# A two-layer RWKV-7 / RG-LRU trunk: the triangular solves on two engines, and their loads and merges as steps of their own

## The chip, the cores and the metric

The kernel runs on one core of a Trainium2 chip. The metric is the device time of one execution, in microseconds (us); the figure compared is the median of several executions. The engines are named as in the profile: PE (TensorE), PEld (its weight loads), DVE (VectorE), ACT (ScalarE), POOL (GpSimd) and SP (SyncE, which issues nearly all DMAs here).

## The reference

A decoder trunk of two layers on 1024 positions of width 1024, in float32. Each layer adds a token mixer, a cross attention into 256 memory rows and a squared-ReLU MLP, each between two RMS norms. Layer 0's mixer is an RG-LRU block, layer 1's is RWKV-7 time mixing, and the change lies in that one:

```python
r = (x + xx * mu[0]) @ w_rkv[0]
k = (x + xx * mu[2]) @ w_rkv[1]
v = (x + xx * mu[3]) @ w_rkv[2]
...
a = jax.nn.sigmoid(a0 + (xa @ a1) @ a2)
kk = (k * k_k).reshape(B, S, H, N).astype(jnp.float32)
kk = kk / jnp.maximum(jnp.linalg.norm(kk, axis=-1, keepdims=True), 1e-12)
k = k * (1.0 + (a - 1.0) * k_a)
...
def step(state, inp):
    r_t, w_t, k_t, v_t, a_t, b_t = inp          # a_t = -kk, b_t = kk * a
    sa = jnp.einsum('bhij,bhj->bhi', state, a_t)
    state = (state * w_t[:, :, None, :] + sa[..., None] * b_t[:, :, None, :]
             + v_t[..., None] * k_t[:, :, None, :])
    y_t = jnp.einsum('bhij,bhj->bhi', state, r_t)
    return state, y_t
```

The kernel computes this recurrence in 16 chunks of 64 positions. Within a chunk the part of `sa` that depends on earlier positions of the same chunk is a triangular system; its inverse `X` (64x64 for each of 16 heads and each chunk) is computed ahead of the scan over the chunks.

## The kernel before

Every big product is made three times with parts of the float32 operands (`split`, L193 on ACT and L194 on DVE, makes the high and low part; `mm3`, L294 to L296, the three matmuls). A scheduler orders the instructions of each engine by its own model of their times, within the dependencies of data and buffers, so an engine's order is not that of the code. Each engine and each DMA queue then works strictly in its order. All DMAs named here are issued by SP, in one queue.

The RWKV layer, around 1280 to 2000 us in the profiled execution, goes like this.

- **k, eight feature blocks** `f` = 0 to 7. `decay(f)` makes the decays (L1143 to L1152: among them the scan L1147 on DVE, the store L1151 of the running product `P`, and the copy L1152 of its last column of each chunk on POOL). `fphase` makes the 48 matmuls of 512 columns of block `f` and hands PSUM to `prep` (L1160 to L1175), which evacuates it: L1160 on ACT and L1163 on DVE read PSUM, L1166, L1171 and L1172 are three products of 128x1024 on DVE, L1168 and L1169 make `at`, L1174 and L1175 store two tensors. `sums(f-1)` (L1182 to L1193) adds squares with 16 small matmuls and sends the norms through DRAM into `db` (L1193). `gram(f-1)` (L1204 to L1212) makes 64 products of 64x64, scales them from PSUM by `db` on DVE (L1205) and stores them: `Ld` holds the diagonal 32x32 blocks, `Mod` the others. With 12 more matmuls for the decay that is 60 of 512 columns for a block.
- **r, eight blocks** in seven turns ([0] to [5], then [6, 7]). `early` loads `P` of the block (L1299), `evac_r` multiplies it by PSUM (L1303, DVE) and stores it (L1304). The mixes of `x` (`rwkv_make_mix`, L1041 on ACT, L1042 and L1044 on DVE, and a split of each of four tiles) are made in two halves, one under the last of k and one behind it; the mix of v likewise around the last turn of r.
- **v, eight blocks**, whose evacuation on DVE is L1334, and then the scan over the 16 chunks.

**The triangular part** works on pairs of blocks, `q` = 0 to 3. `solve(q)` loads 128 blocks of 32x32, one on each partition (L1217), sets `xt_` to the identity (L1219, L1220) and makes 31 steps of two operations, L1225 (a product of two broadcast views, 31 to 256 elements) and L1227 (an addition), each of which needs the one before; L1228 turns the result. `solve_store` writes it to DRAM (L1233, L1234). `merge_load` clears a tile `XT` (L1240) and reads the blocks back in another layout (L1246 to L1248, 8 DMAs a block, 16 a pair), `merge` makes the off-diagonal 32x32 blocks (matmuls L1261 and L1268, ACT copies L1263 and L1271) and stores `XT` (L1272).

`aside(step)` decides where these stand in the code: steps 0 to 7 come at the end of the turns of k, 8 to 14 of r, 15 and later of v. The tuples give for each `q` the step of a function: solves at (2, 5, 7, 10), their stores at (6, 7, 8, 11), the merge's loads at (10, 9, 11, 14) and the merges at (12, 10, 13, 16).

## Time and profile before

| what | value |
|---|---|
| median of 3 executions | 3063.79 us (3063.06 to 3066.52) |
| profiled execution | 3055.81 us, its span 3054.0 us |
| mean granted clock of TensorE | 0.97 |
| busy share of the span | PE 95%, PEld 79%, DVE 59%, ACT 44%, POOL 39% |
| instructions | 42,879 |

The span is the profiled part of one execution, from its first instruction to its last. A busy share is the time in which the engine had an instruction in work; weight loads overlap matmuls. The granted clock is 1 at 2.4 GHz and 0.5 at 1.2 GHz, so a mean between them over a stretch is a mixture of spells at either. In rows of a timeline the number behind the start is the duration, "x4" says that four like instructions stand in one row, and the bracket gives the idle time of the engine ahead of it and what ended it. "SPq" rows are the issue of DMAs by SP's queue.

### The profile page before, as it was taken

The page shows a single profiled execution, that of the slowest core. Times are in us where ns is not written, and L with a number is a line of the kernel's source. Part 1 is how long each engine was busy: PE and PEld are TensorE (multiplying, and loading weights), DVE is VectorE, ACT ScalarE, POOL GpSimd, SP SyncE. Part 2 cuts the span into 40 slices and gives each one's busy share as a digit, 9 for nine tenths or more (in the row PEclk, how much of TensorE's full clock was granted, in tenths as well). Part 3 has the DMA queues.
Part 4 walks back from the last instruction along what each step waited for, and adds up shares of the span by engine and source line. Part 5 has one row for each costly group of instructions (what it writes and reads, how often), then busy time and mean ns, then how long its engine had stood idle before and what let it go on. Part 6 is the DMA issues. An engine that isn't in the chain of part 4 may idle for free.

```text
span 3054.0 us, 42879 instructions
## 1 busy us (share of the span) xinstructions
PE 2890.0 (95%) x16987; PEld 2399.1 (79%) x16987; DVE 1788.2 (59%) x1967; ACT 1341.6 (44%) x1907; POOL 1186.4 (39%) x1096
## 2 busy tenths in 40 slices
PE   7999999898999999989977898989999899999998
PEld 6887898786888878877766777878778778887886
DVE  5576542637454787767662535884345644568776
ACT  5464342635454543346331434442334544454332
POOL 2000100015766754440677504662001466667442
PEclk9999999998999999999978999999999999999999
DMA  8213270122545554342537779862312244455443
GB/s 259 71 42 103 83 225 35 56 83 76 169 152 191 211 185 155 104 138 74 134 104 200 208 219 250 176 159 87 107 34 84 83 151 151 153 204 200 158 137 117
DMA packets 394921, 421.93 MB, mean 138 GB/s; under 512 B 103536, under 2 KB 305504, under 8 KB 394720
## 3 DMA queue, kind: packets, MB, share of 16 engines
q1 hardware_dynamic: 384720, 384.96, 42.2%
q0 software_dynamic: 9536, 33.64, 2.8%
q8 instruction: 134, 2.20, 0.3%
q14 instruction: 67, 0.55, 0.1%
q10 hardware_dynamic: 464, 0.59, 0.1%
HBM read 284.31 MB, written 134.74 MB: 137 GB/s over the span
## 4 chain that ended last, share of the span: by engine, by line
PE 49%; POOL 10%; DVE 5%; issue 5%; DMA 2%; ACT 2%; SPq 1%; POOLq 0%; DVEq 0%; ACTq 0%
PE q L294 12%; PE q L295 12%; PE q L296 12%; PE p L295 4%; PE p L296 4%; PE p L294 4%; POOL u L1227 3%; POOL u L1225 2%; DVE u L194 2%; DMA u<-d 1%; POOL u L1542 1%; ACT u L193 1%; PE q L1444 1%; DMA u<-in_b_w_rkv 1%; DVE u L1555 1%
## 5 line engine op out<-in xcount | busy, mean ns | idle before, releaser
L194 DVE TENSOR_TENSOR u<-u,u 128x1024 fp32r<-128x1024 f32 (+1 forms) x518 | 808.3, 1588 | 383.0 <-ACT u L193 358.0
L193 ACT CAST u<-u 128x1024 fp32r<-128x1024 f32 (+1 forms) x550 | 542.7, 1024 | 475.7 <-PE q L295 159.1
L294 PE MATMUL p<-u,u 128*128 128x512 f32 (+1 forms) x1920 | 720.1, 378 | 25.6 <-ACT u L193 12.2
L295 PE MATMUL p<-u,u 128*128 128x512 f32 (+1 forms) x1920 | 722.5, 376 | 9.2 <-DVE u L194 9.2
L296 PE MATMUL p<-u,u 128*128 128x512 f32 (+1 forms) x1920 | 719.8, 375 | 3.7 <-DVE u L194 3.7
L294 PE MATMUL q<-u,u 128*128 128x512 f32 (+1 forms) x1632 | 643.6, 395 | 39.1 <-DVE u L1205 16.7
L295 PE MATMUL q<-u,u 128*128 128x512 f32 (+1 forms) x1632 | 640.1, 393 | 6.2 <-DVE u L194 6.2
L296 PE MATMUL q<-u,u 128*128 128x512 f32 (+1 forms) x1632 | 634.9, 392 | 0.0
L294 PEld LDWEIGHTS p<-u,u 128*128 128x128 f32 x1920 | 369.4, 193 | 95.2 <-ACT u L193 17.0
L295 PEld LDWEIGHTS p<-u,u 128*128 128x128 f32 x1920 | 370.3, 193 | 77.1 <-DVE u L194 13.7
L296 PEld LDWEIGHTS p<-u,u 128*128 128x128 f32 x1920 | 370.0, 193 | 68.9 <-DVE u L194 5.8
L305 POOL TENSOR_SCALAR s<-s 128x1 f32<-128x1 f32 x98 | 34.4, 351 | 994.6 <-ACT u L303 993.6
L294 PEld LDWEIGHTS q<-u,u 128*128 128x128 f32 (+1 forms) x1632 | 308.9, 190 | 111.7 <-DVE u L1205 17.1
L295 PEld LDWEIGHTS q<-u,u 128*128 128x128 f32 (+1 forms) x1632 | 309.5, 190 | 71.8 <-DVE u L194 8.1
L296 PEld LDWEIGHTS q<-u,u 128*128 128x128 f32 (+1 forms) x1632 | 309.2, 189 | 65.3 <-issue 0.4
L421 POOL TENSOR_TENSOR u<-u,u 128x1024 f32<-128x1024 f32 x64 | 179.1, 2820 | 86.5 <-DVE u L194 80.4
L965 DVE TENSOR_TENSOR z<-z,q 128x512 f32<-128x512 f32 x192 | 128.7, 679 | 93.4 <-PE q L296 93.1
L194 POOL TENSOR_TENSOR u<-u,u 128x1024 fp32r<-128x1024 f32 x32 | 95.0, 2967 | 165.0 <-ACT u L193 104.0
L401 POOL TENSOR_TENSOR u<-u,u 128x512 f32<-128x512 f32 x96 | 148.2, 1553 | 2.9
L294 PE MATMUL q<-z,u 128*128 128x512 f32 x256 | 102.1, 399 | 7.0 <-DVE u L600 7.0
L916 POOL TENSOR_TENSOR u<-u,u 128x512 f32<-128x512 f32 x32 | 46.1, 1440 | 158.5 <-ACT u L905 152.4
L1225 POOL TENSOR_TENSOR u<-u,u 128x31 f32<-128x31 f32 (+15 forms) x124 | 84.9, 685 | 53.0 <-DMA u<-d 32.4
(251 smaller groups left out, 3500.0 us busy)
## 6 DMA issues: line engine op xcount, KB each, us to landing
u<-d SPq DMA_DIRECT2D x201, 512.0 KB, 4.4
d<-u SPq DMA_DIRECT2D x113, 512.0 KB, 3.5
d<-u SPq DMA_DIRECT2D x132, 256.0 KB, 3.5
u<-in_m_w_up SPq DMA_DIRECT2D x64, 512.0 KB, 5.8
d<-u POOLq DMA_DIRECT2D x64, 512.0 KB, 4.1
u<-in_m_w_down SPq DMA_DIRECT2D x64, 512.0 KB, 6.4
u<-in_c_w_kv SPq DMA_DIRECT2D x32, 512.0 KB, 6.5
u<-d SPq DMA_DIRECT2D x56, 256.0 KB, 6.1
```

What stands on the lines that cost most here:

```text
L193: self.nc.scalar.copy(hv, src)
L194: (eng or self.nc.vector).tensor_tensor(lv, src, hv, ALU.subtract)
L294: mm(o, ah, bh, start=first, stop=False, **kw)
L295: mm(o, ah, bl, start=False, stop=False, **kw)
L296: mm(o, al, bh, start=False, stop=last, **kw)
L305: nc.gpsimd.tensor_scalar(v, ss, 1.0 / n, eps, ALU.mult, ALU.add)
L401: sub = lambda o, x, y: nc.gpsimd.tensor_tensor(o, x, y, ALU.subtract)
L421: self.nc.gpsimd.tensor_tensor(f[o][i], f[x][i], f[y][i], ALU.subtract)
L916: tt(s1, r21, r22, ALU.add)
L965: nc.vector.tensor_add(to_, to_, o)
L1225: nc.gpsimd.tensor_tensor(tv, xv_[:, 0:n, s:s + 1].broadcast_to([128, n, m]), Lv[:, s:s + 1, s + 1:].broadcast_to([128, n, m]), ALU.mult)
L1227: nc.gpsimd.tensor_tensor(xv_[:, 0:n, s + 1:], xv_[:, 0:n, s + 1:], tv, ALU.add)
```

## The change

Three of the four solves, `q` = 1 to 3, go from POOL to DVE with all their operations; `q` = 0 stays on POOL (`SE`). `solve` is cut in two: `solve_load` (the load and the two memsets) and `solve`. The store of `XT` leaves `merge` and becomes `merge_store`. Each call in `aside` stands under `behind()`, which takes the last instruction in the code so far on each engine and lets the scheduler issue the call's instructions only after it. The steps are new numbers, and later ones for the stores of the solves of `q` = 0 to 3: (12, 10, 12, 14). Besides, the three products of `prep` (L1166, L1171, L1172) go from DVE to POOL, the copy L1152 from POOL to ACT, and the memset of `XT` (L1240) from POOL to DVE.

```diff
--- before.py
+++ after.py
...
+    @contextmanager
+    def behind(self):
+
+        with ExitStack() as stack:
+            if not self.rec:
+                last = {i.engine: i for i in self.nc.cur_bb.bb.instructions}
+                for i in last.values():
+                    stack.enter_context(self.tc.issue_after(i))
+            yield
 
 
     def nm(self, s):
@@ -980,7 +990,10 @@
                     rest()
 
 
-SO, ST, ML, ME = (2, 5, 7, 10), (6, 7, 8, 11), (10, 9, 11, 14), (12, 10, 13, 16)
+
+SL, SO, ST = (6, 7, 9, 11), (7, 8, 10, 12), (12, 10, 12, 14)
+ML, ME, MS = (13, 11, 13, 15), (14, 12, 14, 16), (15, 13, 15, 17)
+SE = [lambda nc: nc.gpsimd] + [lambda nc: nc.vector] * 3
 DA = (2, 1)
 LD = 6
 POST = lambda nc: nc.vector
@@ -1129,7 +1142,7 @@
     nc.gpsimd.memset(d01[:, ::64], 0.0)
     ch = lambda t: t.rearrange("p (c t) -> p c t", t=64)
     hr = [slice(0, 64), slice(64, 128)]
-    dk, st_k, mg, sol, ld, sm = {}, {}, {}, {}, {}, {}
+    dk, st_k, mg, sol, ld, sm, xts = {}, {}, {}, {}, {}, {}, {}
 
     def decay(f):
         cs = slice(f * 128, f * 128 + 128)
@@ -1149,7 +1162,7 @@
         nc.scalar.activation(P, IP, AF.Exp)
         nc.scalar.activation(IP, IP, AF.Exp, scale=-1.0)
         nc.sync.dma_start(Pd[cs, :], P)
-        nc.gpsimd.tensor_copy(self.pc.rearrange("p (c q) -> p c q", q=8)[:, :, f], P[:, 63::64])
+        nc.scalar.copy(self.pc.rearrange("p (c q) -> p c q", q=8)[:, :, f], P[:, 63::64])
         dk[f] = a, P, IP
 
     def prep(f, pk):
@@ -1163,13 +1176,13 @@
         nc.vector.tensor_mul(kp, kp, pk)
         sq = self.unit()
         nc.scalar.activation(sq, kk, AF.Square)
-        nc.vector.tensor_mul(a, a, kk)
+        nc.gpsimd.tensor_tensor(a, a, kk, ALU.mult)
         at = kk
         nc.vector.scalar_tensor_tensor(ch(at)[:, :, 1:], ch(kk)[:, :, 1:], -1.0, ch(P)[:, :, :63], ALU.mult, ALU.mult)
         nc.vector.tensor_scalar(at[:, ::64], kk[:, ::64], -1.0, None, ALU.mult)
         nc.sync.dma_start(MVd[:, f, 0, :], at)
-        nc.vector.tensor_mul(a, a, IP)
-        nc.vector.tensor_mul(kp, kp, IP)
+        nc.gpsimd.tensor_tensor(a, a, IP, ALU.mult)
+        nc.gpsimd.tensor_tensor(kp, kp, IP, ALU.mult)
         for h in range(2):
             nc.sync.dma_start(STd[hr[h], f, h, :], a[hr[h], :])
             nc.sync.dma_start(STd[hr[h], f, 1 - h, :], kp[hr[h], :])
@@ -1211,33 +1224,36 @@
                 nc.sync.dma_start(Ld[f // 2, b, f % 2, h].rearrange("c s t -> s c t"), ch(mt)[rs, :, b * 32:b * 32 + 32])
             nc.sync.dma_start(Mod[f, h], ch(mt)[h * 64:h * 64 + 32, :, 32:64])
 
+    def solve_load(q):
+        sol[q] = [self.unit() for _ in range(3)]
+        L, xt_, tmp = sol[q]
+        nc.sync.dma_start(L, Ld[q].rearrange("b q h c s t -> (b q h c) (s t)"))
+        SE[q](nc).memset(xt_, 0.0)
+        SE[q](nc).memset(xt_[:, ::33], 1.0)
+
     def solve(q):
 
-        L, xt_, tmp = (self.unit() for _ in range(3))
-        nc.sync.dma_start(L, Ld[q].rearrange("b q h c s t -> (b q h c) (s t)"))
+        L, xt_, tmp = sol[q]
+        eng = SE[q](nc)
         Lv = L.rearrange("p (s t) -> p s t", t=32)
-        nc.gpsimd.memset(xt_, 0.0)
-        nc.gpsimd.memset(xt_[:, ::33], 1.0)
         xv_ = xt_.rearrange("p (j t) -> p j t", t=32)
         for s in range(31):
             n, m = s + 1, 31 - s
             tv = tmp[:, :n * m].rearrange("p (j t) -> p j t", t=m)
-            nc.gpsimd.tensor_tensor(tv, xv_[:, 0:n, s:s + 1].broadcast_to([128, n, m]),
-                                    Lv[:, s:s + 1, s + 1:].broadcast_to([128, n, m]), ALU.mult)
-            nc.gpsimd.tensor_tensor(xv_[:, 0:n, s + 1:], xv_[:, 0:n, s + 1:], tv, ALU.add)
-        nc.gpsimd.tensor_copy(tmp[0:64].rearrange("p (s j) -> p s j", j=32), xt_[0:64].rearrange("p (j s) -> p s j", s=32))
-        sol[q] = xt_, tmp
+            eng.tensor_tensor(tv, xv_[:, 0:n, s:s + 1].broadcast_to([128, n, m]),
+                              Lv[:, s:s + 1, s + 1:].broadcast_to([128, n, m]), ALU.mult)
+            eng.tensor_tensor(xv_[:, 0:n, s + 1:], xv_[:, 0:n, s + 1:], tv, ALU.add)
+        eng.tensor_copy(tmp[0:64].rearrange("p (s j) -> p s j", j=32), xt_[0:64].rearrange("p (j s) -> p s j", s=32))
 
     def solve_store(q):
-        xt_, tmp = sol.pop(q)
+        L, xt_, tmp = sol.pop(q)
         nc.sync.dma_start(Xd[q].rearrange("b q h c s t -> (b q h c) (s t)"), xt_)
         nc.sync.dma_start(Xnd[2 * q:2 * q + 2].rearrange("q h c s t -> (q h c) (s t)"), tmp[0:64])
-
 
     def merge_load(q):
         for f in (2 * q, 2 * q + 1):
             XT = self.unit()
-            nc.gpsimd.memset(XT, 0.0)
+            nc.vector.memset(XT, 0.0)
             XN = self.unit()
             xc = ch(XT)
             for h in range(2):
@@ -1269,13 +1285,19 @@
                        start=True, stop=True, tile_position=(h * 64 + 32, h * 64))
             for h in range(2):
                 nc.scalar.copy(xc[r0[h], :, 32:64], ps[r0[h], :].rearrange("p (c t) -> p c t", t=32))
-            nc.sync.dma_start(XTd[:, f, :], XT)
+            xts[f] = XT
+
+    def merge_store(q):
+        for f in (2 * q, 2 * q + 1):
+            nc.sync.dma_start(XTd[:, f, :], xts.pop(f))
 
     def aside(step):
 
-        for fn, steps in ((solve_store, ST), (merge, ME), (merge_load, ML), (solve, SO)):
-            if step in steps:
-                fn(steps.index(step))
+        for fn, steps in ((merge_store, MS), (merge, ME), (merge_load, ML), (solve_store, ST), (solve, SO), (solve_load, SL)):
+            for q in range(4):
+                if steps[q] == step:
+                    with self.behind():
+                        fn(q)
 
     self.depth, self.ahead = DA
     xr, xv = [], []
```

The lines of the changed kernel have other numbers: L1225 and L1227 (solve) become L1243 and L1245, L1219 and L1220 (its memsets) L1231 and L1232, L1217 (its load) L1230, L1233 and L1234 (its store) L1250 and L1251, L1240 (memset of `XT`) L1256, L1246 to L1248 (loads of the merge) L1262 to L1264, L1193 (`db`) L1206, L1205 (`gram`) L1218, L1299 (load of `P`) L1321, L1303 (evacuation of r) L1325, L1304 L1326, L194 L204, L225 (weights) L235.

First place: SP's queue in the last turns of k. In the kernel before, the store of solve 0 (L1233, L1234) stands there ahead of loads of `db` (L1193):

```order
L1233 DMA d_10006<-u_10824 128x1024
L1151 DMA d_10001<-u_11214 128x1024
L1234 DMA d_10007<-u_10825 64x1024
L1193 DMA db<-d_11325 64x8 x2
L1175 DMA d_10003<-u_11310 64x1024 x2
L1170 DMA d_10002<-u_11308 128x1024
L1193 DMA db<-d_11325 64x8
```

In the changed kernel the queue of the same turns reads as follows (`d_11417` is the DRAM copy of the norms, `d_10005` is `Ld`, `d_10004` is `Mod`):

```order
L1164 DMA d_10001<-u_11306 128x1024
L1206 DMA db<-d_11417 64x8 x4
L1183 DMA d_10002<-u_11400 128x1024
L1188 DMA d_10003<-u_11402 64x1024 x2
L1224 DMA d_10005<-u_11424 32x16x32 x2
L1225 DMA d_10004<-u_11424 512x1x32
L1187 DMA d_10003<-u_11307 64x1024 x2
```

The stores of a solve are gone from there: the first of them, solve 1's, stands in the turns of r, 40 rows further down, and solve 0's behind r4's load of `P`. The `db` loads now follow a store of `P` (L1164) that needs only ACT.

Second place: DVE in the turns of r. Before, only the evacuations (L1303) and the splits of the weights (L194) stand there:

```order
L1303 TENSOR_TENSOR u_12039<-u_12039,p_12047 128x1024
L194 TENSOR_TENSOR u_12125<-u_12041,u_12124 128x1024
L1303 TENSOR_TENSOR u_12120<-u_12120,p_12128 128x1024
L194 TENSOR_TENSOR u_12417<-u_12122,u_12416 128x1024
L1303 TENSOR_TENSOR u_12412<-u_12412,p_12420 128x1024
```

In the changed kernel the operations of solves 1 to 3 stand between the evacuations. The rows below are the end of solve 1 and the evacuation of r4; `u_12024` is the `xt_` of solve 2, `u_12235` that of solve 3:

```order
L1243 TENSOR_TENSOR u_12025<-u_12024,u_12023 128x31
L1245 TENSOR_TENSOR u_12024<-u_12024,u_12025 128x31
L1246 COPY u_12025<-u_12024 64x1024
L1231 MEMSET u_12235 128x1024
L1232 MEMSET u_12235 128x32
L204 TENSOR_TENSOR u_12245<-u_12155,u_12244 128x1024
L1325 TENSOR_TENSOR u_12240<-u_12240,p_12248 128x1024
L1243 TENSOR_TENSOR u_12236<-u_12235,u_12234 128x31
L1245 TENSOR_TENSOR u_12235<-u_12235,u_12236 128x31
```

Ahead of r2's evacuation there are 20 rows since r1's, ahead of r3's 33, and ahead of r4's (the L1325 above) 79, nearly all of them operations of solves 1 and 2.

Third place: SP's queue around the first merge loads. Before, those of solve 1 enclose r2's load of `P`, and the store of solve 2 stands among them (`u_12120` is r2's tile):

```order
L1247 DMA u_12111<-d_10007 32x16x32
L1248 DMA u_12111<-d_10004 32x512
L1299 DMA u_12120<-d_10001 128x1024
L225 DMA u_12122<-in_b_w_rkv 128x8x128
L1247 DMA u_12323<-d_10007 32x16x32
L1248 DMA u_12323<-d_10004 32x512
L1247 DMA u_12323<-d_10007 32x16x32
L1246 DMA u_12321<-d_10006 32x16x32 x3
L1233 DMA d_10006<-u_11807 128x1024
L1304 DMA d_10002<-u_12120 128x1024
```

In the changed kernel (`u_12240` is r4's tile, `u_12506` r5's):

```order
L1262 DMA u_12223<-d_10006 32x16x32 x2
L1263 DMA u_12225<-d_10007 32x16x32
L1264 DMA u_12225<-d_10004 32x512
L1230 DMA u_12234<-d_10005 128x1024
L1321 DMA u_12240<-d_10001 128x1024
L235 DMA u_12242<-in_b_w_rkv 128x8x128
L1321 DMA u_12506<-d_10001 128x1024
L235 DMA u_12508<-in_b_w_rkv 128x8x128
L1326 DMA d_10002<-u_12240 128x1024
L1250 DMA d_10006<-u_11468 128x1024
```

The merge loads of solve 1 (L1262 to L1264) moved behind r2's and r3's loads of `P`; with the load of solve 3 (L1230) they now stand in one piece ahead of r4's. Behind these rows 32 merge loads of solves 0 and 2 stand ahead of the loads of `P` of r6 and r7.

## Rows read from the trace of the kernel before

**Rows 1.** The page: busy time, share of the span and instructions of each engine

```profile
PE 2890.0 (95%) x16987; PEld 2399.1 (79%) x16987; DVE 1788.2 (59%) x1967; ACT 1341.6 (44%) x1907; POOL 1186.4 (39%) x1096
```

**Rows 2.** Windows: stretch, length, busy PE, PEld, DVE, ACT, POOL, granted clock, DMA share, GB/s

```profile
1422.20:1550.40 128.20, 111.49 (x763) 89.56 (x762) 80.57 (x88) 45.02 (x54) 64.48 (x85) 0.85 0.56 154
1550.40:1584.80 34.40, 30.50 (x214) 23.41 (x213) 30.16 (x30) 18.96 (x24) 32.28 (x32) 0.85 0.34 89
1584.80:1622.20 37.40, 25.35 (x153) 19.15 (x152) 22.83 (x33) 8.85 (x11) 32.49 (x47) 0.87 0.41 111
1622.20:1727.20 105.00, 91.32 (x1057) 74.06 (x1058) 33.53 (x31) 33.94 (x48) 78.47 (x114) 0.85 0.71 193
1727.20:1748.90 21.70, 21.70 (x96) 17.66 (x95) 15.55 (x22) 9.56 (x12) 3.63 (x2) 1.00 1.04 265
```

**Rows 3.** Waits from 1300 to 1860 us: total us, times, longest

```profile
SPq L1233 <- POOL u L1227: 55.7, 3, 29.7
...
DVE u L1303 <- DMA u<-d: 43.5, 4, 21.3
```

**Rows 4.** Timeline of SP's queue: the store that holds up k5

```profile
1526.73 0.34 SPq L1233 DMA_DIRECT2D d<-u  x1
```

**Rows 5.** Timeline of DVE: two waits of L1205

```profile
1538.85 1.29 DVE L1205 TENSOR_TENSOR u<-q,db 128x512 f32<-128x512 f32 x2 [20.61 <-DMA db<-d]
...
1619.37 1.29 DVE L1205 TENSOR_TENSOR u<-q,db 128x512 f32<-128x512 f32 x2 [7.31 <-DMA db<-d]
```

**Rows 6.** Timeline of PE: sums, Gram product, and two big matmuls 25 rows apart

```profile
1507.76 1.84 PE L1182 MATMUL q<-ind,u 128*128 128x2 f32 x16
1509.54 2.08 PE L1204 MATMUL q<-u,u 64*64 64x64 f32 x64
...
1724.76 0.39 PE L296 MATMUL p<-u,u 128*128 128x512 f32 x1
...
1730.65 0.39 PE L295 MATMUL p<-u,u 128*128 128x512 f32 x1
```

**Rows 7.** Timeline of ACT: the evacuation of k1

```profile
1430.06 1.12 ACT L1160 ACTIVATE u<-p,colt 128x1024 f32<-128x1024 f32 x1 [3.51 <-PE p L296]
```

**Rows 8.** Durations on POOL, ns (min/median/max), first and last start: a product of 128x1024

```profile
L421 POOL TENSOR_TENSOR u<-u,u x64: 2377/2415/3407, 1015.3 to 2966.2; 128x1024 f32<-128x1024 f32 x64
```

**Rows 9.** Durations and timeline of POOL: operations of the solves

```profile
L1227 POOL TENSOR_TENSOR u<-u,u x124: 250/652/2559, 1471.8 to 1716.1; 128x31 f32<-128x31 f32 x8, 128x60 f32<-128x60 f32 x8, 128x87 f32<-128x87 f32 x8, 128x112 f32<-128x112 f32 x8
...
1515.63 1.44 POOL L1225 TENSOR_TENSOR u<-u,u 128x207 f32<-128x207 f32 x1
...
1518.78 0.55 POOL L1225 TENSOR_TENSOR u<-u,u 128x192 f32<-128x192 f32 x1
```

**Rows 10.** Durations and timeline of DVE: operations of the preparation

```profile
L1163 DVE TENSOR_TENSOR u<-u,p x8: 1203/1220/1222, 1422.2 to 1584.8; 128x1024 f32<-128x1024 f32 x8
...
1426.21 1.20 DVE L1168 SCALAR_TENSOR_TENSOR u<-u,u 128x1008 f32<-128x1008 f32 x1
1427.33 0.18 DVE L1169 TENSOR_SCALAR u<-u 128x16 f32<-128x16 f32 x1
1427.41 1.22 DVE L1171 TENSOR_TENSOR u<-u,u 128x1024 f32<-128x1024 f32 x1
...
1514.99 1.63 DVE L1168 SCALAR_TENSOR_TENSOR u<-u,u 128x1008 f32<-128x1008 f32 x1
```

**Rows 11.** Timeline of DVE: the scan of the decay

```profile
1429.15 2.28 DVE L1147 TENSOR_TENSOR_SCAN u<-u,u 128x1024 f32<-128x1024 f32 x1
```

**Rows 12.** Timeline of SP's queue: first and last rows of 12 merge loads in succession

```profile
1641.36 0.95 SPq L1246 DMA_DIRECT2D u<-d  x2
...
1647.02 0.49 SPq L1248 DMA_DIRECT2D u<-d  x1
```

**Rows 13.** Timeline of DVE: splits of the r mix, the first and the last two of four

```profile
1596.25 1.23 DVE L194 TENSOR_TENSOR u<-u,u 128x1024 fp32r<-128x1024 f32 x1 [1.17 <-ACT u L193]
...
1609.55 2.50 DVE L194 TENSOR_TENSOR u<-u,u 128x1024 fp32r<-128x1024 f32 x2 [1.17 <-ACT u L193]
```

More of the change, by code (lines that the diff above doesn't have):

```diff
@@ L1 @@
-from contextlib import ExitStack
+from contextlib import ExitStack, contextmanager
 import concourse.bass as bass
```

## The prediction

> **What bounds the kernel now.** I read the page first: PE is busy for 95% of the span [rows 1], so time can only be won where PE stands still or runs at its low clock. The table by stretch is cut at the evacuations of the RWKV layer [rows 2]: k0's (L1163, start 1422.2), k6's (1550.4), k7's (1584.8), r0's (L1303, 1622.2), r7's (1727.2) and v0's (L1334, 1748.9). In the first four stretches PE is busy for 259 of 305 us and its clock is granted at 0.85 to 0.87, against 1.00 in the fifth: the stretches hold spells at 1.2 GHz among those at 2.4. So what this change can touch holds some 46 us of still PE, and low clock on top.
>
> Next the waits show who holds PE. SyncE's queue waited 55.7 us for POOL's solve (L1227) before it could issue L1233, the store of a solve [rows 3]. The queue is in order, and `db` loads stand behind that store. The one that holds up k5 goes out at 1526.73 [rows 4], `db` loads behind it; VectorE's L1205 waited 20.61 us for them and started at 1538.85, and later waited 7.31 us for the `db` of k7 [rows 5]. L1205 frees the PSUM banks of the Gram product that PE needs next. That is the chain: POOL solve, store, queue, `db`, L1205, PE.
>
> **What a k step costs without that chain.** PE does 60 products of 512 columns for a feature block. 26 of them start between 1724.76 and 1730.65, 0.2265 us each, so 13.6 us; the Gram product takes 2.08 and the sums 1.84 us [rows 6]. Sum 17.5 us. k1's evacuation begins on ScalarE at 1430.06 [rows 7], before any solve runs, and the order up to there is nearly the same in both programs, so it stays. Five more evacuations follow at 17.5 us; the VectorE part of an evacuation begins 1.1 us behind ScalarE's: k6 at 1430.1 + 5 x 17.5 + 1.1 = 1518.7, against 1550.4. **Term 1: -31.7 us.**
>
> The cover for it is that VectorE and POOL fit into 17.5 us. The three products that move (L1166, L1171, L1172) take 1.13 us each from VectorE and 2.42 each from POOL, the median of L421, which has their shape [rows 8]: 7.25 us a step. The two engines shut each other out: POOL takes 0.55 us for 192 elements while VectorE rests and 1.44 for 207 while it works [rows 9]; VectorE's L1168 goes from 1.20 to 1.63 us, but L1163, which reads PSUM, stays within 1.203 to 1.222 [rows 10]. The Trainium skill, GPSIMD Engine Reference, section 8, says the same: contention with VectorE instructions that have two SBUF inputs. What VectorE keeps that shuts POOL out is L1168 1.1, the scan L1147 2.2 [rows 11], the split L194 1.1, three operations with one tensor input (L1144, L1145, L1162; I take 0.65 each) and small ones 0.3: an estimate of 6.7 in all. With POOL's 7.25 that is 13.9; L1163, two L1205 and the reciprocal, 2.7, need not exclude POOL. At most 16.7 us, under 17.5. If that cover fails, each step is longer by the excess.
>
> From k6's to k7's evacuation VectorE and ScalarE carry the r mix and bound the step, 34.4 us. Three products leave VectorE, 3 x 1.13 = 3.4; POOL's products take the place of solve operations that filled 32.3 of those us [rows 2]. **Term 2: -3.4 us**, bounds 0 and -6. From k7's to r0's evacuation the 7.31 us wait for `db` [rows 5] goes, since POOL's solve 0 is stored only after r4; the second half of the r mix stays as it is. **Term 3: -7.3 us.** Together -42.4 at r0's evacuation. The copy L1152 moves to ScalarE, which is busy for 45 of 128 us there; the memsets of XT move to VectorE (no row shows a VectorE memset; between 0.6 and 1.1 us each, I take 0.8): they are in the next term.
>
> **The r stretch, 105.0 us now.** It had 43.5 us of L1303 waiting for loads of P behind stores and merge loads [rows 3]. After, VectorE carries three solves. One is 62 operations on 5,456 x 2 elements. For 16 elements VectorE takes 0.18 us and for 1024 1.22, so 0.16 us fixed and 1.03 ns an element: 0.34 for the mean 176. Where one does not read the other's result, the next starts 0.08 us after L1169's start, 0.10 before its end [rows 10]. I take 0.37 in a dependent chain and 0.28 where two solves alternate. In the order the evacuations stand between the solve's operations, so VectorE is late by what lies in front:
> (a) Before r2's evacuation 17 operations. POOL's solve 0 runs beside them; one for one, an operation costs 0.34 + 0.6 = 0.97 us [rows 9]. With a memset and a split 19 us, against 10.9 of PE.
> (b) Before r3's, 32 more, a third beside POOL: 9.7 + 6.6 + split and evacuation 3 = 19.3. Now at 3 + 19 + 1 + 19 = +42, PE was ready at +22.
> (c) Before r4's, 72 operations, two copies, three memsets and the split of r6: 52 x 0.29 + 20 x 0.33 + 6 = 28, +70. The P load of r4 stands behind 14 merge loads of solve 1 (12 take 6.2 us [rows 12]) and their landing: +77.
> (d) r6 and r7 are 21.8 us on PE, +99; solve 3 is 58 x 0.37 + 3 from +81; the P loads of r6 and r7 stand behind 32 merge loads, 16.5 us, some of which wait for memsets inside solve 3: r7's evacuation at +111.
> So +111 if the engines alternate one for one, **+6 us**; without exclusion (a) and (b) are hidden and every later step comes earlier, near PE's own pace: +87, **-18**. I take **term 4: 0**, nearer the alternation, which rows 9 and 10 show.
>
> **Then the v mix.** Before, its first half lies under r6 and r7; after, its L1042 stand behind r7's evacuation, as solve 3 fills that place. Four tiles: 1596.25 to 1609.55 is three of them, 4.4 us each [rows 13]. **Term 5: +17 us** (16 to 18). From v0 on PE is the bound in both.
>
> **Sum:** -31.7 - 3.4 - 7.3 + 0 + 17 = -25.4. The profiled execution took 3055.8 us (span 3054.0 and 1.8 around it), so 3030; it ran 8 us under the median of the three runs, 3063.8, on whose scale I give the forecast: **3038 us.**
>
> **Rivals.** First, exclusion is weak for such short operations: term 4 is -18 and the time 3020. For it: POOL's L1227 has its median at 0.65 us [rows 9], over a time in which VectorE was at work for much of it. Against it: L1168's 1.63 [rows 10].
>
> Second, the move of the products costs what it should bring. VectorE waits 2.42 us for each instead of doing it in 1.13, in series with everything: 17.5 becomes 13.6 (VectorE's step before) - 3.4 + 7.25 + 2 of waiting on POOL's results = 19.5, so five steps lose 10 us and term 2 turns to +2: 3053. Against it: 2.7 us can overlap and PE's 17.5 is long. The Trainium skill, GPSIMD Engine Reference, section 4.1, puts elementwise work on VectorE, GpSimd being about twice as slow with two inputs; the rows agree (2.42 in rows 8 against 1.22 in rows 10), and by that rule alone this rival would be the forecast.
>
> Third, slower than before: the solve's operations are dear on VectorE. They have rows of 1 to 31 elements and broadcast inputs, which no row of VectorE shows; POOL's median for the same shapes is 0.65 us [rows 9]. Some 183 of them lie on the path, so 0.1 us more each is 18 us. From 0.17 more (a mean of 0.5 instead of 0.33) the kernel is slower by over 0.2%; at 0.6, POOL's level, it is 183 x 0.27 = +49, less 25: 3088. For it: three solves of 62 dependent short operations now sit in the queue that evacuates PSUM. The Trainium skill, VectorE: DVE Perf Modes, section on the TRN2 errata, warns of a fixed cost per SBUF instruction and advises tiles of 512 elements or more; the 0.18 us for 16 elements [rows 10] agrees in kind.
>
> Fourth, the change moves the blockage without a gain: queue waits for solve 1's store and its merges cost in r what they cost in k. The +77 and +111 already hold most of that; a worse case is 3058, within 0.2%.
>
> **Chances.** Forecast 0.5, weak exclusion 0.2, dear products 0.13, blockage moved 0.07, dear solve 0.10. A measurement here tells about 0.2% (6 us) from no change: faster 0.80, the same 0.10, slower 0.10. The range: low, terms 1 to 3 at their bounds (-45), term 4 -18, term 5 +16: -47, 3017, and 4 for the runs; high, the moved blockage and most of the dear products: 3060.
>
> **What would show it.** Right: no wait of `db` over 3 us in the k steps; k6's evacuation near 1519 and r0's near 1580; POOL's products with a median near 2.5; VectorE's solve operations near 0.3 to 0.4 beside a resting POOL, near twice that beside a busy one; PE still for some 15 us before r6; the v mix behind r7's evacuation. Wrong: k steps over 18.5 us; solve operations of 0.5 us without POOL; or merges and P loads that reach PE early.

## The result: slower by 0.22%, and the profile after

The changed kernel took 3071.34 us (median of 20 runs, 3067.93 to 3075.95) against 3063.59 for the kernel before (20 runs): ratio 1.0022, interval 1.0015 to 1.0028. Forecast was 3038. The profiled execution spans 3072.8 us, 18.8 more than before; the medians differ by 7.8, because the execution profiled of before was a quick one and that of the changed kernel lies 3 us above its median. The stretches below are compared between the profiles.

The page's busy row, which answers to [rows 1]:

```profile
PE 2889.2 (94%) x16987; PEld 2394.9 (78%) x16987; DVE 1864.2 (61%) x2146; ACT 1344.2 (44%) x1915; POOL 1098.1 (36%) x909
```

The table by stretch, which answers to [rows 2], cut at the same evacuations (k0, k6, k7, r0, r7, v0; then v2 and v3):

```profile
1425.80:1535.10 109.30, 104.16 (x781) 84.37 (x781) 81.88 (x71) 47.68 (x61) 48.76 (x18) 0.95 0.56 148
1535.10:1567.20 32.10, 27.55 (x195) 20.55 (x192) 25.10 (x27) 18.82 (x25) 10.09 (x6) 0.93 0.57 147
1567.20:1597.30 30.10, 27.13 (x154) 20.52 (x152) 22.53 (x33) 10.97 (x14) 28.21 (x29) 0.85 0.55 154
1597.30:1700.60 103.30, 77.09 (x608) 63.18 (x608) 87.92 (x205) 8.82 (x12) 27.50 (x37) 0.86 0.59 163
1700.60:1742.20 41.60, 33.82 (x544) 25.96 (x544) 28.89 (x46) 32.51 (x46) 3.62 (x2) 0.85 0.62 171
1742.20:1762.70 20.50, 19.47 (x86) 14.72 (x86) 10.82 (x13) 7.72 (x11) 0.00 (x0) 1.00 0.60 148
1762.70:1793.90 31.20, 24.05 (x98) 18.29 (x97) 6.16 (x8) 4.27 (x6) 0.00 (x0) 0.89 0.87 232
```

| stretch | before | after | difference | forecast |
|---|---|---|---|---|
| up to k0 | 1422.2 | 1425.8 | +3.6 | 0 |
| k0 to k6 | 128.2 | 109.3 | -18.9 | -31.7 |
| k6 to k7 | 34.4 | 32.1 | -2.3 | -3.4 |
| k7 to r0 | 37.4 | 30.1 | -7.3 | -7.3 |
| r0 to r7 | 105.0 | 103.3 | -1.7 | 0 |
| r7 to v0 | 21.7 | 41.6 | +19.9 | +17 |
| v0 to the scan's first chunk | 110.2 | 131.7 | +21.5 | 0 |
| from there on | | | +4.0 | 0 |

The scan's first chunk is taken at the same matmul, 1859.02 before (L1444) and 1873.85 after (L1466). v0 is taken at its evacuation, L1334 before and L1356 after; that is a copy on ScalarE, not on VectorE. Up to r7 the change had won 26.6 us; the v mix and the v blocks gave back 41.4.

**Where k lost.** Timelines of GpSimd and VectorE behind k0's evacuation, and PE's wait ahead of k2:

```profile
1428.15 2.88 POOL L1185 TENSOR_TENSOR u<-u,u 128x1024 f32<-128x1024 f32 x1
1430.98 3.34 POOL L1184 TENSOR_TENSOR u<-u,u 128x1024 f32<-128x1024 f32 x1
...
1428.69 3.41 DVE L1181 SCALAR_TENSOR_TENSOR u<-u,u 128x1008 f32<-128x1008 f32 x1
1432.02 2.34 DVE L1182 TENSOR_SCALAR u<-u 128x16 f32<-128x16 f32 x1
...
1448.66 0.79 PE L304 MATMUL q<-u,u 64*128 64x512 f32 x1 [5.14 <-DVE u L1218]
```

The operation that becomes L1182 works on 16 elements and took 0.18 us in [rows 10]; here it takes 2.34, and ends with the product that GpSimd ran meanwhile (L1184). L1181 and L1182 together held VectorE for 5.7 us in place of 1.3. The decay's scan stands behind them, so k1 comes at 1439.94, 14.2 us after k0 (11.2 before); in the next step L1218 stands behind them, and PE waits.

From k2 on every step takes 18.26 us. L1182 is held there too (2.38 us), but PE itself is the bound, as the window of one step shows (busy PE 18.26 of 18.26, clock 1.00):

```profile
1516.83:1535.09 18.26, 18.26 (x148) 14.82 (x144) 13.86 (x12) 8.10 (x10) 8.06 (x3) 1.00 0.61 162
```

Within that step the first two big matmuls behind a pair of the small `sums` matmuls (L1195) start 0.32 us apart, and the next one 0.23 us behind:

```profile
1530.08 0.28 PE L1195 MATMUL q<-ind,u 128*128 128x2 f32 x2
1530.21 0.48 PE L304 MATMUL p<-u,u 128*128 128x512 f32 x1
1530.53 0.40 PE L305 MATMUL p<-u,u 128*128 128x512 f32 x1
1530.76 0.39 PE L306 MATMUL p<-u,u 128*128 128x512 f32 x1
```

**Where the v blocks lost.** Timelines of SyncE's queue, VectorE and PE ahead of v2:

```profile
1763.83 4.41 SPq L1292 DMA_DIRECT2D d<-u  x4
1768.36 2.42 SPq L1262 DMA_DIRECT2D u<-d  x2
...
1777.71 0.48 SPq L1264 DMA_DIRECT2D u<-d  x1
1778.29 0.37 SPq L1390 DMA_DIRECT2D u<-d  x1
...
1785.50 1.28 DVE L1358 SCALAR_TENSOR_TENSOR u<-u,colt,u 128x1024 f32<-128x1024 f32 x1 [20.58 <-DMA u<-d]
...
1786.84 2.08 PE L1377 MATMUL q<-u,ones 128*128 128x512 f32 x2 [7.14 <-DVE u L1358]
```

Four stores of `XT` and the 16 loads of the merge of solve 3 stand ahead of v2's loads (L1390) for 14.5 us; VectorE waits 20.58 us and PE 7.14.

**Where the v mix stands.** Timelines of SyncE and ScalarE around r7:

```profile
1695.07 0.90 SPq L1321 DMA_DIRECT2D u<-d  x2
1696.01 1.06 SPq L235 DMA_DIRECT2D u<-in_b_w_rkv  x2
...
1702.40 1.05 ACT L203 CAST u<-u 128x1024 fp32r<-128x1024 f32 x1 [24.83 <-DMA u<-in_b_w_rkv]
1703.35 1.33 ACT L1054 ACTIVATE u<-z,omu 128x512 f32<-128x512 f32 x2
```

The load of v0's weights (L235) stands behind 32 merge loads and the loads of `P`; its split waits for it on ScalarE, and the mix (L1054) stands behind the split.

### The profile page after: what moved, and what is told of

Its sections match the earlier page's. It is cut to its first block, busy times and chain, and to the rows that moved or that the text cites. A ratio compares the mean times of both kernels' runs of the same rounds, so it can differ in the third digit from the quotient of the medians.

```text
span 3072.8 us, 42865 instructions
## 1 busy us (share of the span) xinstructions
PE 2889.2 (94%) x16987; PEld 2394.9 (78%) x16987; DVE 1864.2 (61%) x2146; ACT 1344.2 (44%) x1915; POOL 1098.1 (36%) x909
## 4 chain that ended last, share of the span: by engine, by line
PE 54%; DVE 8%; issue 5%; POOL 4%; ACT 2%; DMA 2%; SPq 1%; POOLq 0%; DVEq 0%; ACTq 0%
PE q L304 12%; PE q L305 12%; PE q L306 12%; PE p L304 4%; PE p L305 4%; PE p L306 4%; DVE u L204 3%; PE q L1466 1%; ACT u L203 1%; DVE u L1245 1%; DVE u L1243 1%; DMA u<-d 1%; POOL u L1564 1%; PE q L1377 1%; DVE u L1577 1%
## 5 line engine op out<-in xcount | busy, mean ns | idle before, releaser
L204 DVE TENSOR_TENSOR u<-u,u 128x1024 fp32r<-128x1024 f32 (+1 forms) x518 | 812.2, 1596 | 351.4 <-ACT u L203 335.0
L204 POOL TENSOR_TENSOR u<-u,u 128x1024 fp32r<-128x1024 f32 x32 | 95.1, 2971 | 166.3 <-ACT u L203 104.2
L411 POOL TENSOR_TENSOR u<-u,u 128x512 f32<-128x512 f32 x96 | 150.8, 1579 | 2.9
L610 DVE SCALAR_TENSOR_TENSOR u<-p,s,u 128x1024 f32<-128x1024 f32 x24 | 30.8, 1284 | 122.3 <-ACT u L203 78.2
L204 DVE TENSOR_TENSOR u<-p,u 128x1024 fp32r<-128x1024 f32 x32 | 38.9, 1221 | 108.6 <-ACT u L203 108.6
```

The source lines that it names most:

```text
L204: (eng or self.nc.vector).tensor_tensor(lv, src, hv, ALU.subtract)
L411: sub = lambda o, x, y: nc.gpsimd.tensor_tensor(o, x, y, ALU.subtract)
L610: nc.vector.scalar_tensor_tensor(o, src, r, gb, ALU.mult, ALU.mult)
```

## The experiments

Theory A came first: k lost through the products on GpSimd, v through the place of merge 3's loads, the mix through solve 3 on VectorE. Where a run shows another cause, it is named D below. Medians are compared with 3071.3; ratios are to runs of the kernel before that were taken beside each experiment.

**1. The products back on VectorE** (L1179, L1184, L1185):

```diff
-        nc.gpsimd.tensor_tensor(a, a, kk, ALU.mult)
+        nc.vector.tensor_mul(a, a, kk)
```

> The three products of prep go back to VectorE, all else as in the changed kernel. Theory A (the products on GpSimd cost the start of k, because a VectorE instruction with SBUF operands that meets one waits for its end; the 16-element L1182 took 2.34 and 2.31 us there): L1182 is back at about 0.2 us, the evacuations of k1 and k2 (VectorE part) come near 1434 and 1452 in place of 1439.9 and 1462.0, k6 near 1523 in place of 1535.1, the r mix behind it grows by about 3 us, and the time falls by 8 to 11 us, to about 3061 (ratio to before 0.998 to 1.000). Theory B (k is late through PE's own order, with the sums split up): k6 stays within 3 us of 1535 and the ratio at 1.002 or above.

3059.9 us, ratio 0.9987 (0.9979 to 0.9996). As expected: L1182 is back at 0.18 us, and k6 comes 100.3 us after k0 in place of 109.3. The 9.0 us lie in the first three steps (k0 to k3 takes 45.5 us in place of 54.6); from k3 on a step takes 18.25 to 18.27 us here too. Then the r mix gives back 2.2 and k7 to r0 3.0, and r0 to r7 takes 95.7 us in place of 103.3, which was not expected. Of these 7.6 us, 7.5 lie between r1 and r3. What differs there: GpSimd's solve 0 stood behind k7's products. In the changed kernel its products (L1243) start from 1570.9 to 1624.9, beside VectorE's solves, here from 1541.2 to 1596.6, almost clear of them. No run moved solve 0 alone. The solve's L1245 alone in windows (length, busy VectorE and GpSimd with their counts, clock, DMA), of the changed kernel:

```profile
1597.20:1625.20 28.00, 10.34 (x20) 11.29 (x18) 1.00 0.55 165
1625.20:1656.00 30.80, 15.26 (x42) 0.34 (x1) 0.87 0.27 66
```

and of this run:

```profile
1596.80:1640.00 43.20, 17.84 (x56) 0.27 (x1) 1.00 0.42 127
```

Beside GpSimd one takes 0.52 us (10.34 / 20), without it 0.36 and 0.32. The windows hold different sizes; over the eleven sizes from 31 to 231 elements that the changed kernel ran both ways, the means are 0.58 and 0.31 us.

**2. The 16-element operation alone to ScalarE:**

```diff
-        nc.vector.tensor_scalar(at[:, ::64], kk[:, ::64], -1.0, None, ALU.mult)
+        nc.scalar.mul(at[:, ::64], kk[:, ::64], -1.0)
```

> Only L1182, the negation of 16 elements a partition, moves from VectorE to ScalarE; the products stay on GpSimd. Theory A: VectorE comes free 2.2 us earlier in k0 and k1, so k1 comes about 2 us earlier (1437.8) and PE's wait for L1218 before k2 falls from 5.1 to about 3 us; later k steps stay at 18.26 us, since PE is the bound there; the time falls by 3 to 5 us, to about 3067. Theory B: nothing moves by more than 1 us.

3066.4 us, ratio 1.0012 (1.0003 to 1.0021): 4.9 us for eight operations of 16 elements. PE's wait ahead of k2 is the one expected. But k1 gained nothing: it comes 14.09 us after k0 in place of 14.19, and it stands near the expected time only because k0 was 1.8 us earlier in this profile. The decay's scan now stands where L1182 stood, is held by the same product of GpSimd and takes 4.45 us in place of 2.28. Timelines of VectorE and PE:

```profile
1430.20 4.45 DVE L1160 TENSOR_TENSOR_SCAN u<-u,u 128x1024 f32<-128x1024 f32 x1
...
1443.80 0.68 DVE L1218 TENSOR_TENSOR u<-q,db 128x512 f32<-128x512 f32 x1
...
1444.53 0.79 PE L304 MATMUL q<-u,u 64*128 64x512 f32 x1 [3.03 <-DVE u L1218]
```

L1218, one of whose inputs lies in PSUM, takes 0.68 us though GpSimd's product runs from 1442.78 to 1446.11. So the next step does gain, 20.7 us in place of 22.1.

**3. The loads of merge 3 on GpSimd's queue:**

```diff
-                    nc.sync.dma_start(xc[rs, :, b * 32:b * 32 + 32], Xd[q, b, f % 2, h]...)
+                    (nc.gpsimd if q == 3 else nc.sync).dma_start(xc[rs, :, b * 32:b * 32 + 32], Xd[q, b, f % 2, h]...)
```

(and the two loads behind it likewise).

> Only the 16 loads of the merge of solve 3 leave SyncE's queue for GpSimd's; the order on VectorE and on SyncE is otherwise the same but for small moves. Theory A (v is long because these loads stand ahead of v2's loads in SyncE's queue): v2's loads are issued near 1769 in place of 1778.3, PE's wait of 7.1 us for L1358 and the low clock behind it go, and v0 to the first chunk of the scan falls from 131.7 us to 115 to 119; the time falls by 12 to 17 us, to about 3057 (ratio 0.995 to 0.998). Theory B (the DMA engines themselves are full in v, at a share of 0.87 to 1.00): the loads take the same time from v2's whoever issues them, and the time falls by less than 4 us.

3063.2 us, ratio 0.9995 (0.9986 to 1.0004): 8.2 us, between the two theories. v2's loads go out at 1766.75, 11.5 us earlier, but L1358 still waits 15.37 us: the four stores stand ahead of the loads as before, and the DMA share is 1.00 and 1.04 in 1762:1770 and 1770:1778; v0 to the scan falls from 131.7 to 123.3.

**4. Both together:**

> Products back on VectorE and the loads of merge 3 on GpSimd's queue. Theory A: the two losses lie in different stretches and add, so the time falls by 20 to 27 us from the changed kernel, to about 3048 (ratio 0.993 to 0.996). Theory B: less than 5 us.

3052.5 us, ratio 0.9960 (0.9947 to 0.9972): 18.8 us less than the changed kernel, where 11.4 and 8.2 make 19.6. The two losses add.

**5. Solve 3 on GpSimd:**

```diff
-SE = [lambda nc: nc.gpsimd] + [lambda nc: nc.vector] * 3
+SE = [lambda nc: nc.gpsimd, lambda nc: nc.vector, lambda nc: nc.vector, lambda nc: nc.gpsimd]
```

> The changed kernel with solve 3 back on GpSimd (solves 1 and 2 stay on VectorE); SyncE's order is the same. Theory A (the v mix is late because solve 3 fills VectorE's place under r6 and r7): the first half of the v mix is done under r6 and r7, r7 to v0 falls from 41.6 to 22 to 27 us, and the time falls by 12 to 18 us, to about 3056. Theory B (solve 3 on GpSimd, 62 operations of 0.65 us from about 1663, ends later than 1706.8 and holds SyncE's queue at its store, ahead of v0's loads, and shuts VectorE out in r): the gain is under 5 us.

3067.6 us, ratio 1.0004 (0.9995 to 1.0013), and r7 to v0 still 42.1 us (1697.86 to 1739.92). Theory A falls for the mix: from r5 to r7 VectorE is busy for only 7.7 us of 31.4 (24.7 of 32.5 in the changed kernel), and ScalarE waits as before:

```profile
1699.68 1.04 ACT L203 CAST u<-u 128x1024 fp32r<-128x1024 f32 x1 [24.74 <-DMA u<-in_b_w_rkv]
1700.64 0.72 ACT L1054 ACTIVATE u<-z,omu 128x512 f32<-128x512 f32 x1
```

**6 and 7. The loads of merge 3 and the store of solve 3 one step earlier, with the products on VectorE, and with solve 3 on GpSimd as well:**

```diff
-SL, SO, ST = (6, 7, 9, 11), (7, 8, 10, 12), (12, 10, 12, 14)
-ML, ME, MS = (13, 11, 13, 15), (14, 12, 14, 16), (15, 13, 15, 17)
+SL, SO, ST = (6, 7, 9, 11), (7, 8, 10, 12), (12, 10, 12, 13)
+ML, ME, MS = (13, 11, 13, 14), (14, 12, 14, 16), (15, 13, 15, 17)
```

> The products on VectorE (as in the first experiment, 3059.9 us), and the loads of merge 3 one step earlier (step 14 in place of 15, the store of solve 3 at 13), so that they stand in SyncE's queue ahead of v0's loads, where the queue is idle during the v mix (1714 to 1737 in the changed kernel). Theory A (their place in the queue ahead of v2's loads costs the time in v): v0 to the first chunk of the scan falls from 126 to about 112 to 117 us, v0 itself stays within 3 us, and the time is 3046 to 3051. Theory C (what is left in v comes from the four stores of XT and from the merge on ScalarE, which stay where they are): no better than the run with the loads on GpSimd's queue and the products on VectorE, 3052 or more.

> All three together: products on VectorE, solve 3 on GpSimd, loads of merge 3 at step 14. Theory A: the gains lie in k, in the v mix and in v and add up: 3059.9 - 14 (v mix) - 10 (v) = 3036 us, 3032 to 3042. Theory B (solve 3 on GpSimd ends too late for its store and loads, which now stand ahead of v0's loads): 3045 or more, with a wait of SyncE's queue for GpSimd at that store.

The first: 3045.2 us, ratio 0.9931 (0.9919 to 0.9944), v0 to the scan 116.3 us (1729.52 to 1845.82). So the place of these loads is worth 14.7 us on top of the products; theory C falls. v0 to the scan wins 13.7 us by it (130.0 in run 1), and r7 to v0 loses 6.6 of them (47.8, 41.3 in run 1): the loads now stand ahead of a load of v's weights, and ScalarE waits for that just ahead of v0:

```profile
1728.45 1.04 ACT L203 CAST u<-u 128x1024 fp32r<-128x1024 f32 x1 [6.52 <-DMA u<-in_b_w_rkv]
```

The second: 3047.8, ratio 0.9936 (0.9922 to 0.9949); solve 3 on GpSimd brings nothing here either. Its theory B had the time right, but not the reason: the queue waits for GpSimd at that store for at most 1.6 us.

**8. The kernel before with only its stores of the solves pinned later:**

```diff
-SO, ST, ML, ME = (2, 5, 7, 10), (6, 7, 8, 11), (10, 9, 11, 14), (12, 10, 13, 16)
+SO, ST, ML, ME = (2, 5, 7, 10), (9, 8, 10, 13), (10, 9, 11, 14), (12, 10, 13, 16)
...
-                fn(steps.index(step))
+                if fn is solve_store:
+                    with self.behind():
+                        fn(steps.index(step))
+                else:
+                    fn(steps.index(step))
```

> The kernel before, with nothing changed but the stores of solves 0 to 3 pinned to later steps (9, 8, 10, 13): all solves and merges stay on GpSimd and VectorE keeps the products. It shows what the store of solve 0 ahead of the loads of db cost. Theory A: the wait of 20.6 us for db goes, k6 comes near 1525 in place of 1550.4 and r0's evacuation 24 to 30 us earlier than 1622.2; in r the loads of P wait for the later stores and merge loads, so about half is given back: 3046 to 3055 us (ratio 0.994 to 0.998). Theory B (k is slow because the solves on GpSimd shut VectorE out): k6 stays later than 1540 and the ratio at 0.998 or above.

3051.4 us, ratio 0.9949 (0.9937 to 0.9962). VectorE's timeline (L1215 is before's L1205, L1317 its L1303) shows 4.26 us where it waited 20.61 [rows 5], and what the later stores cost in r:

```profile
1523.70 0.69 DVE L1215 TENSOR_TENSOR u<-q,db 128x512 f32<-128x512 f32 x1 [4.26 <-DMA db<-d]
...
1644.13 1.22 DVE L1317 TENSOR_TENSOR u<-u,p 128x1024 f32<-128x1024 f32 x1 [38.09 <-DMA u<-d]
```

All waits for `db` come to 16.4 us, the longest 6.3 (40.0 and 20.6 before). k6 comes 111.1 us after k0 (128.2 before), at 1535.1, where 1525 was expected. The chain of solve, store, queue and `db` was real, and cutting it alone is worth more than the whole change.

**9. The loads of merges 0 and 2 on GpSimd's queue** (the edit of 3 with `q in (0, 2)`):

> The changed kernel with the 32 loads of the merges of solves 0 and 2 on GpSimd's queue in place of SyncE's; solve 3 stays on VectorE. In the run with solve 3 on GpSimd the v mix still took 42 us, so solve 3 on VectorE is not what makes it late. Theory D (the load of r7's weights stands behind these 32 loads in SyncE's queue; its split waited 24.8 us for it on ScalarE, and the v mix stands behind that split): the loads of P and weights go out some 25 us earlier, r5 to r6 falls from 31.2 to 20 to 25 us, r7 to v0 from 41.6 to 25 to 32 us, the time falls by 18 to 25 us, to about 3049. Theory A of before (solve 3 on VectorE holds the mix up): r7 to v0 stays over 38 us, and the gain is under 10 us.

3066.0 us, ratio 1.0004 (0.9995 to 1.0012). r5 to r6 falls to 19.2 us, as expected, but r7 to v0 does not: it takes 45.0. (The weights behind the 32 loads are those of v0, not of r7: r7's evacuation, at 1700.59 in the changed kernel, starts before they have landed.) The mix starts at 1688.80, 14.6 us earlier, but v0 comes only 6.5 earlier, at 1735.64: solve 3's last operations on VectorE (its store goes out at 1707.43) and copies of merges 0 and 2 on ScalarE now lie among the mix, and from its start to v0 it takes 46.8 us in place of 38.8. Which of the two costs more was not tried.

**10. All four solves on GpSimd** (`SE = [lambda nc: nc.gpsimd] * 4`):

> The changed kernel with all four solves on GpSimd; steps, products and queues as changed. Four solves of 62 operations of 0.65 us in a row from 1571 end near 1735, and the stores hold SyncE's queue. Theory A (the solves had to leave GpSimd for the new, late steps to be bearable): r7's evacuation 25 us or more later than 1700.6, the time 3090 or more. Theory B (VectorE's solves bring nothing, as the merges are pinned late anyway): within 8 us of 3071.

3115.3 us, ratio 1.0168 (1.0154 to 1.0182). The solves end at 1746, and SyncE's queue waits 58.9 us for them at their stores (total, times, longest):

```profile
SPq L1250 <- POOL u L1245: 58.9, 3, 36.7
```

With these late steps the move of three solves to VectorE is worth 44 us.

**11 and 12. The edits of 1, 6 and 9 together, then with all 64 merge loads on GpSimd's queue:**

> Products on VectorE, loads of merge 3 at step 14 (together 3045.2 us), and the loads of merges 0 and 2 on GpSimd's queue. Theory D: another 18 to 24 us less, 3021 to 3028 us. Theory A of before: 3036 or more.

> As the combination above, but all 64 loads of the merges on GpSimd's queue. Theory D: those of solve 1 ahead of r4's load of P cost some 6 us of queue and those of solve 3 are in an idle stretch, so 0 to 6 us less than the combination with 32 loads: 3018 to 3026 us. Against it: GpSimd's own issue of a load takes longer (0.5 to 0.7 us a load in the run with merge 3 on it), and the merge of solve 1 may come later.

3036.2 us, ratio 0.9909 (0.9896 to 0.9922), and 3037.4, ratio 0.9910 (0.9897 to 0.9923). Nine us less than run 6, half of what was expected: as in run 9 the mix starts earlier (1672.6, 1684.4 in run 6) and takes longer, and r7 to v0 is 48 us, as in run 6. Both are faster than the two kernels of this case by some 0.9 and 1.1%.

**13 and 14. The first half of the v mix in r5's turn, in the changed kernel and in the combination of 11:**

```diff
-        if len(fs) > 1:
+        if fs[0] == 5:
             self.later.append(lambda: xv.append(rwkv_make_mix(self, X, 3, 0)))
```

> The changed kernel with the first half of the v mix put into the turn of r5 in place of that of r6 and r7; on ScalarE it then stands ahead of the split of v0's weights, which waited 24.8 us for its load. Theory D (v0 comes some 39 us after the mix starts, and the mix could not start before that load had landed, whatever VectorE had to do): the first half is done by 1700, r7 to v0 falls from 41.6 to 22 to 28 us, the time falls by 12 to 18 us, to about 3056. Theory A (solve 3 on VectorE leaves no room for the mix under r6 and r7, so it only pushes solve 3 and its store back): r7 to v0 stays over 36 us, the gain is under 5 us.

> The same edit in the combination with products on VectorE, loads of merge 3 at step 14 and loads of merges 0 and 2 on GpSimd's queue (3036.2 us; there r7 to v0 is 48 us). Theory D: the first half of the mix is done before r7, r7 to v0 falls to 28 to 36 us, the time falls by 10 to 18 us, to 3018 to 3026. Theory A: 3032 or more.

3072.5 us, ratio 1.0033 (1.0020 to 1.0046), and 3041.9, ratio 0.9928 (0.9915 to 0.9941): nothing gained by the first, and 5.7 us lost by the second against run 11. In run 13 r7 to v0 fell to 35.1 us, not to the 22 to 28 of theory D, and r7 itself came 5 us later: the mix pushed the memsets of `XT` on VectorE back, the merge loads waited for those, and the loads of `P` for r6 and r7 stand behind them. Timelines of VectorE and SyncE in run 13:

```profile
1685.13 0.91 DVE L1256 MEMSET u<- 128x1024 f32 x1 [0.16 <-issue]
...
1679.64 0.42 SPq L1263 DMA_DIRECT2D u<-d  x1
1686.08 2.96 SPq L1262 DMA_DIRECT2D u<-d  x6
...
1699.90 0.90 SPq L1321 DMA_DIRECT2D u<-d  x2
```

**15 and 16. Merges 0 and 2 without their compute, then without their loads too:**

```diff
             XN, XT = mg.pop(f)
+            if q in (0, 2):
+                xts[f] = XT
+                continue
...
-            for h in range(2):
+            for h in range(0 if q in (0, 2) else 2):
                 for b in range(2):
```

> The changed kernel without the small matmuls and ScalarE copies of the merges of solves 0 and 2 (their loads and stores stay; the inverse of these blocks is then incomplete). Theory M (these merges, on PE and ScalarE between r5 and v0, set that stretch, 74.1 us from r5's to v0's evacuation in the changed kernel, 55.5 before): it falls under 62 us and the time by 12 us or more. Theory S (the load of v0's weights behind the 32 merge loads, and the mix behind it, set it): it stays over 70 us and the time within 5 us of 3071.

> As the run without the compute of merges 0 and 2, and without their 32 loads too. Theory S: the weights of v0 are loaded some 25 us earlier, the mix starts near 1680, r5 to v0 falls to 52 to 60 us, and the time by 14 to 22 us, to 3050 to 3057. Theory V (solve 3 and the mix together fill VectorE in this stretch, whatever the queue does): r5 to v0 stays over 64 us.

3065.6 us, ratio 1.0008 (0.9998 to 1.0017), and 3048.8, ratio 0.9954 (0.9939 to 0.9969). Both kernels leave part of the inverse `X` out. From r5 to v0 it is 68.1 and 50.4 us (74.1 in the changed kernel): the merges' compute is worth 6.0 us of this stretch, the 32 loads 17.7. Without the loads the stretch is shorter than it was before (55.5). In run 16 the mix starts at 1678.93 and v0 (L1359 in this kernel) comes 38.3 us later:

```profile
1678.93 0.72 ACT L1054 ACTIVATE u<-z,omu 128x512 f32<-128x512 f32 x1
...
1717.24 1.01 ACT L1359 COPY u<-p 128x1024 f32<-128x1024 f32 x1
```

The distance is 38.8 in the changed kernel, 39.3 in run 5 and 35.3 in run 15. Theory D (S in these expectations) holds in the main: v0 follows the start of the mix, and that follows v0's weights, behind the 32 loads. Run 9 sets its limit: with these loads on another queue the mix itself takes longer.

## Why the prediction was wrong, step by step

Between the two profiles the forecast was -25.4 us, and +18.8 came. Of the 44.2 us between them 21.5 lie behind v0, where the prediction saw no change, and 12.8 in term 1.

**What bounds the kernel, and the chain of solve, store, queue and `db`:** right. Run 8 cut it alone and won 0.5%.

**Term 1, -31.7:** measured -18.9 as a length from k0: the forecast had 96.5 us from k0 to k6, and it took 109.3, 12.8 more. Run 1 divides that: 9.0 us come with the three products on GpSimd, 3.8 are there without them. Three steps failed.

- "The order up to there is nearly the same in both programs, so it stays": the order stayed, but operations in between were held by GpSimd, which run 1 prices at 9.0 us up to k3. L1182 was counted among "small ones 0.3" and takes 2.3 us or more in each of the steps to k6.
- "the VectorE part of an evacuation begins 1.1 us behind ScalarE's": for k1 it began 3.3 us behind already in the kernel before (1433.38 against 1430.06), as VectorE first worked through the decay's scan and a split. k0 to k1 is 11.2 us before and in run 1, where the forecast had 9.0.
- PE's step is 18.26 us, not 17.5. The sum took 0.2265 us for every big matmul; in the trace the first ones behind each change between them and the small ones (and between those of the block and of the decay) are 0.31 to 0.34 us apart. The three steps from k3 to k6 make 2.3 us by that, with the products on either engine.

These make 13.5 us, and in run 1 the steps from k1 to k3 take 0.6 us less than forecast. The cover of 16.7 under 17.5 us did hold in the steady step; it was not there in k0 and k1, where the decay's scan and L1218 stood right behind the held operations. (The time of k6, 1535.1 for a forecast of 1518.7, holds 3.6 us more, by which k0 itself was late.)

**The second rival** (the products cost what they should bring) had the size, 9.0 us up to k6 for 10, but not the mechanism: no steady step grew. Taking the move back is worth 11.4 us, the 9.0 in the first steps and 7.6 in r, where the products had pushed solve 0 back by 30 us, less 5.2 that the r mix gives back.

**Terms 2 and 3:** -2.3 and -7.3, for -3.4 and -7.3: right in size. Term 2's reason held too: with the products back, run 1 gives up 2.2 us. Term 3's wait for `db` is gone, but in run 1, where it is gone as well, the stretch is only 4.3 us shorter than before; 3.0 of the 7.3 came with the products, which the term did not count.

**Term 4, 0:** -1.7. That VectorE and GpSimd hold each other up was right, the price was not: 0.52 us an operation beside GpSimd where the prediction had 0.97 (its 0.34 + 0.6 makes 0.94), 0.36 without. r3 came 33.0 us after r0, where alternation was to make 42, and r7 103.3 after, for 111; so 0, taken between the two bounds, was in part luck. The solve's operations have medians of 0.376 (L1243) and 0.389 us (L1245) on VectorE, for 0.37 forecast; the third rival falls.

**Term 5, +17:** measured 19.9, so the size is right, by luck. The step named the wrong cause: "as solve 3 fills that place". Run 5 emptied the place and nothing moved; run 16 shows that v0's weights gate the mix. The list under (d) had the `P` loads behind the 32 merge loads, and not the weights that stand behind those.

**"From v0 on PE is the bound in both":** this failed outright, by 21.5 us, the largest miss. The merge of solve 3 had moved one step, to 15, and with it 16 loads and four stores came to stand between v1's and v2's loads. Run 6 shows 13.7 us of it as the place of the loads (130.0 to 116.3 us); the rest, the stores and the merge's copies on ScalarE, was not tried by itself. The fourth rival, the moved blockage, is what happened, but in v, where the prediction priced it in r at a few us.

The terms do not cover the 3.6 us ahead of k0 and 4.0 us in the scan; the times of k0 in the other profiles lie between 1421.4 and 1426.2, so the first is not shown to be an effect of the change. What makes the second was not looked into.

## What to carry to other kernels

Follow every DMA of a moved step to the queue row that it lands in, in the stage behind the one that you mean to help, and ask of each transfer behind it (weights too) who waits for it. Before giving an elementwise operation to GpSimd, look for what stands next on VectorE: even an operation of 16 elements can wait there for the end of a 2.4 us product, and if you move that one away, the next with two inputs from SBUF waits in its place (run 2). Where one blocked queue entry is the loss, try moving that entry alone: it won 0.5% here, while the change lost 0.2%.

## What the runs showed of the hardware

The exclusion of VectorE and GpSimd was stricter for single operations than [rows 9, 10] had led to expect: the two took turns, operation by operation. A VectorE operation of 16 elements with one input took 2.34 us in place of 0.18 beside a product of GpSimd (L1184), and that product 3.34 in place of 2.41, its own time and the 1 us that it waited for L1181. With that operation on ScalarE the scan took 4.45 us in place of 2.28. Two VectorE operations that read PSUM were not held: L1176 took 1.21 to 1.22 us beside L1179, and L1218 0.68. The Trainium skill, GPSIMD Engine Reference, section 8, names VectorE operations with two SBUF inputs or in the two-port mode as those that contend; the rows of L1181 and of the scan agree. L1182 has one input, so by that section only the two-port mode is left for it, and no run here shows the mode.
